# Causal mask by GpSimd and VectorE, two attention value products regrouped: one fused two-layer kernel

## The chip, the cores and the metric

The kernel runs on one core of one Trainium2 chip as a single program. The metric is device time in microseconds (us). Engines are named as in the profile: PE (TensorE matmuls), PEld (its weight loads), DVE (VectorE), ACT (ScalarE), POOL (GpSimd), SP (SyncE, which here only issues DMAs).

## The reference, cut to what matters

Two blocks follow each other on 1024 tokens of width 1024 (plus 16 meta tokens in the first). The first block runs a state space branch (SSD) and a "forgetting attention" (fox) of 16 heads of 64 side by side. The second runs a differential attention (4 heads, values 128 wide) and a dilated attention (8 heads of 64). The change touches the three attentions:

```python
# fox: q, k, v per head; c is the running sum of log forget gates
s = q @ k.T * scale + (c_q[:, None] - c_k[None, :])
s = where(kpos[None, :] <= qpos[:, None], s, -inf)      # causal mask
o = softmax(s) @ v
# differential: two score maps per head, no mask
w = softmax(s0 - slope * dist) - lam * softmax(s1 - slope * dist)
o = w @ v                                               # v is 128 wide
# dilated: windows of dilation 1, 4, 16, merged by their denominators
o = sum over patterns of (window softmax) @ v
```

## The kernel before

All work is hand-ordered: generators yield pieces of attention, and a fixed table (RATIOS, ORDERS, the planner in `merge`) puts projection matmuls between them. Each engine then runs its own instructions strictly in the order written, so a wait of one instruction holds all that is queued behind it on that engine. Projections and scores are split: a fp32 value is held as hi (fp32r, a faster matmul type) plus lo, and a product is two or three fp32r matmuls (`mm3`, L112 to L114, is hi·hi, hi·lo and lo·hi).

Stages in the trace: 0 to 76 us prologue, 76 to 645 fox (8 pairs of heads, some 71 us each with their filler), 645 to 1430 SSD, 1430 to 1815 the merge of the first block, 1815 to 2190 differential (4 heads, some 90 us each), 2190 to 2510 dilated (4 pairs of heads), and then the tail.

An attention loop over eight query tiles i of 128 rows runs as a software pipeline (`pipeline`): `pre(i)`, `A(i+2)`, `C(i-1)`, `B(i)`.

- **A** computes scores. In fox, for each head j of the pair: per bank, matmuls of the hi and lo keys (L566, L567), then a bf16 matmul of an identity with a mask table that adds the causal mask to the last 128 columns (L569), then one DVE instruction that adds the bias `cb` and takes the running minimum into `mn` (L570, printed as CUSTOM_DVE_ANT_0, with a READ_ACCUMULATOR behind it), then the exp on ACT with that minimum as bias (L573), then a copy of 16 columns on POOL (`pm`, L576). Tile i is 16 + 128(i+1) columns wide, N is the tile's scores.
- **B** transposes the tile on PE (L624) and copies it out of PSUM into `pt` (L630 on ACT; fox and differential use ACT, dilated alternates with DVE, L632).
- **C** multiplies by the values. In fox it runs once per four tiles (L604, L607, with the sum taken out by L609). In differential it runs per tile, eight fp32 128x128 matmuls (L1211; each shows as two instructions). In dilated per tile, ten 64-wide fp32 matmuls (L1318) and one of 96 rows (L1319) for leftover columns, which a DVE copy collects into `more` (L1290) and PE transposes (L1301).

In the differential loop `pre(i)` (L1193 to L1195) forms the difference of the two exps of tile i on DVE; A has two 1024-wide reductions (L1173) and two exps (L1176). `vtok` are the values by tokens (L469), evacuated by ACT. The gate `zs` of a fox pair is a projection in the filler that ends in a tanh on ACT (L519) and a product on DVE (L520).

Of the kernel before, what the change touches and what calls it, by code (L numbers as in the profile page):

```python
# [66 lines left out]
class Kern:  # L67
# [128 lines left out]
    def consts(self):  # L196
# [6 lines left out]
        self.identb = cst.tile([128, 128], BF16, name="identb")  # L203
        self.maskb = cst.tile([128, 128], BF16, name="maskb")
        V.tensor_copy(out=self.identb, in_=self.ident)
        V.tensor_copy(out=self.maskb, in_=self.cm[:, 3, :])
# [253 lines left out]
    def v_tokens(self, vT, blocks):  # L460

        nc = self.nc
        v = self.slot("vtok", w=1024)
        vv = v.rearrange("p (b c) -> p b c", c=128)
        for g in range(0, len(blocks), 4):
            ps = self.bank()
            for n, c0 in enumerate(blocks[g:g + 4]):
                nc.tensor.transpose(ps[:, n * 128:(n + 1) * 128], vT[:, c0:c0 + 128], self.ident)
            nc.scalar.activation(out=v[:, g * 128:g * 128 + 512], in_=ps, func=AF.Copy)  # L469
        return vv  # L470
# [67 lines left out]
    def fox_attend(self, p, st):  # L538
# [12 lines left out]
        def A(i):  # L551
# [6 lines left out]
            for j in range(2):  # L558
                N = self.slot("N")
                mn = self.sm.tile([128, 3], F32, tag="mn", name="mn", bufs=4)  # L560
                qt = st["q"][j][:, i * 128:(i + 1) * 128]
                for c in range(n):
                    s0, s1 = c * w, min(W, c * w + w)
                    S = self.bank()[:, :s1 - s0]
                    last = c == n - 1
# [7 lines left out]
                nc.scalar.activation(out=N[:, :W], in_=N[:, :W], func=AF.Exp, scale=-1.0, bias=mn[:, n - 1:n],  # L573
# [41 lines left out]

    def transposes(self, N, off, nb, pts, act=False):

        nc = self.nc
        for g in range(0, nb, 4):
# [5 lines left out]
            self.evac(pts[g // 4][:, :n], ps[:, :n * 128].rearrange("p (b c) -> p b c", c=128), act)  # L625
# [35 lines left out]
    def ssd_chunks(self, g, st):  # L661
# [43 lines left out]
        def prep(c):  # L705
# [7 lines left out]
            cbm = self.sm.tile([128, 128], F32, tag="cbm", name="cbm", bufs=2)  # L713
# [402 lines left out]
    def v_by_tokens(self, n, st):  # L1116
        vT = st.pop("vT")
        st["v"] = self.v_tokens(vT, [128 * b for b in range(8)])
        if n >= 4:
            st["vx"] = self.v_more(vT)  # L1120
            next(st["vx"])
        yield
# [56 lines left out]
    def diff_attend(self, p, st):  # L1179
# [18 lines left out]
        def B(i):  # L1198
            P = Ws.pop(i)
            pt = self.slot("pt", w=1024)  # L1200
            r = pt.rearrange("p (b c) -> p b c", c=128)
            self.transposes(P[0], 0, 8, [r[:, :4], r[:, 4:]], act=True)
            PTs[i] = pt
            return 8 * 109

        def C(i):
            pt = PTs.pop(i)
            if i % 4 == 0:
                O[0] = self.bank()
            for b in range(8):  # L1210
                te.matmul(O[0][:, (i % 4) * 128:(i % 4 + 1) * 128], st["v"][:, b, :], pt[:, b * 128:(b + 1) * 128],  # L1211
                          start=b == 0, stop=b == 7)
            if i % 4 == 3:
                nc.scalar.activation(out=y[:, (i - 3) * 128:(i + 1) * 128], in_=O[0], func=AF.Copy)
            return 8 * 218
# [34 lines left out]
    def dil_attend(self, p, st):  # L1250
# [3 lines left out]
        Ns, PTs, O = {}, {}, [None]  # L1254

        def A(i):
            d = dil_tile(i)
            own = d["own"]
            n0, n1 = own.stop - own.start, d["nrest"]
            Ns[i] = []  # L1260
            for j in range(2):
# [3 lines left out]
                q = st["q"][j][:, i * 128:(i + 1) * 128]  # L1265
# [5 lines left out]
                for c, (at, tab, n) in enumerate(((d["own_at"], d["tab_own"], n0), (d["rest_at"], d["tab_rest"], n1))):  # L1271
# [4 lines left out]
                                     accum_out=self.lall[:, 4 + 2 * p + j, i:i + 1])  # L1276
                Ns[i].append(N)
            return 8 * 145

        def B(i):  # L1280
            d = dil_tile(i)
            if i == 0:
                st["vx"] = next(st["vx"])
            big, small = self.slot("pt", w=1024), self.slot("pt", w=512)
            more = self.sm.tile([128, 128], F32, tag="cbm", name="more", bufs=2)[:, :96]
            for j in range(2):
                N = Ns[i][j]
                x = N[:, 256:688] if d["a"] == 0 else N[:, 0:432]
                e = slice(128, 144) if d["a"] == 0 else slice(0, 16)
                V.tensor_copy(out=more[:, 48 * j:48 * j + 48].rearrange("p (c e) -> p c e", e=16),  # L1290
                              in_=x.rearrange("p (c e) -> p c e", e=144)[:, :, e])
                ps = self.bank()
                for b, (_, c) in enumerate(d["blocks"][:4]):
                    te.transpose(ps[:, b * 128:(b + 1) * 128], N[:, c:c + 128], self.ident)
                self.evac(big[:, j * 512:(j + 1) * 512], ps)
                ps = None
            ps = self.bank()
            c = d["blocks"][4][1]
            for j in range(2):
                te.transpose(ps[:, j * 128:(j + 1) * 128], Ns[i][j][:, c:c + 128], self.ident)  # L1300
            te.transpose(ps[:96, 256:384], more, self.ident)  # L1301
            self.evac(small[:, :256], ps[:, :256])
            self.evac(small[:96, 256:384], ps[:96, 256:384])
            PTs[i] = big, small
# [3 lines left out]
        def C(i):  # L1308
            d = dil_tile(i)
            big, small = PTs.pop(i)  # L1310
            if i % 4 == 0:
                O[0] = self.bank()
            q = slice((i % 4) * 128, (i % 4 + 1) * 128)
# [500 lines left out]
```

## Time and profile before

| what | value |
|---|---|
| median of 3 runs | 2732.16 us (2728.64 to 2733.09) |
| profiled execution, its own time | 2729.51 us |
| its span | 2727.7 us |
| PE busy | 2659.8 us, 98% of the span |
| DVE, ACT, POOL busy | 1372.3, 1165.6, 684.5 us (50%, 43%, 25%) |
| mean granted TensorE clock | 0.994 |

PE takes matmuls one behind the other, and their durations overlap, so the price of a matmul is the distance from its start to the next one's start, not the duration printed. The row of a wait gives in brackets how long the engine was idle and who released it. In `2.85 PE L604 ... x16` sixteen instructions are put together in one row.

### The profile page before, as it was taken

The numbers are of one execution on the slowest core, as the hardware profiler recorded it, in microseconds if no ns is written. First come the engines' busy times: TensorE is split into PE (matmuls) and PEld (weight loads), VectorE is DVE, ScalarE is ACT, GpSimd is POOL, SyncE is SP. The second block draws the span as 40 slices with busy tenths as digits, with TensorE's granted clock in tenths as the row PEclk, the third lists the DMA queues.
The fourth block names the chain that finished last, engine by engine and source line by source line (L and its number), as shares of the span: only waits on it lengthen the run. The fifth ranks groups of instructions, "written<-read, shape, count | busy, mean of one in ns | idle before, by whom it ended". The sixth has DMA issues, their size and how long they took to land. (4 is left out here: it accounts for less than half of the span.)

```text
span 2727.7 us, 38674 instructions
## 1 busy us (share of the span) xinstructions
PE 2659.8 (98%) x14925; PEld 2232.2 (82%) x14925; DVE 1372.3 (50%) x2761; ACT 1165.6 (43%) x2080; POOL 684.5 (25%) x764
## 2 busy tenths in 40 slices
PE   8999999999999999999999999999999999998999
PEld 6888888888989889889877887878877877777877
DVE  5433322233574573654756777444654555446332
ACT  5554444445343433443432123445644555445331
POOL 1112121111243342342432333111111121204321
PEclk9999999999999999999999999999999999998999
DMA  3122222221123123122168653340222223324422
GB/s 131 58 64 72 78 79 71 78 64 62 39 88 114 55 78 116 55 103 91 55 207 279 205 182 131 128 121 30 72 70 70 79 94 94 86 72 146 160 65 70
DMA packets 85464, 266.87 MB, mean 98 GB/s; under 512 B 10880, under 2 KB 12032, under 8 KB 84256
## 3 DMA queue, kind: packets, MB, share of 16 engines
q1 hardware_dynamic: 85280, 264.40, 30.3%
q8 instruction: 117, 1.92, 0.3%
q14 instruction: 67, 0.55, 0.1%
HBM read 205.57 MB, written 33.49 MB: 88 GB/s over the span
## 5 line engine op out<-in xcount | busy, mean ns | idle before, releaser
L121 POOL TENSOR_TENSOR wlo<-wraw,whi 128x1024 fp32r<-128x1024 f32 (+2 forms) x168 | 374.4, 2232 | 1288.7 <-ACT whi L120 1077.8
L112 PE MATMUL bank<-uh,whi 128*128 128x512 f32 (+4 forms) x1752 | 625.8, 357 | 0.1
L114 PE MATMUL bank<-uh,wlo 128*128 128x512 f32 (+4 forms) x1752 | 618.8, 353 | 0.1
L113 PE MATMUL bank<-ul,whi 128*128 128x512 f32 (+4 forms) x1752 | 618.5, 353 | 0.0
L114 PEld LDWEIGHTS bank<-uh,wlo 128*128 128x128 f32 (+1 forms) x1752 | 327.9, 187 | 35.4 <-POOL wlo L121 0.5
L112 PEld LDWEIGHTS bank<-uh,whi 128*128 128x128 f32 (+1 forms) x1752 | 328.3, 187 | 34.3 <-issue 1.1
L113 PEld LDWEIGHTS bank<-ul,whi 128*128 128x128 f32 (+1 forms) x1752 | 328.2, 187 | 32.3
L112 PE MATMUL bank<-u,whi 128*128 128x512 f32 x512 | 207.8, 406 | 0.7 <-ACT pr L935 0.7
L113 PE MATMUL bank<-u,whi 128*128 128x512 f32 x512 | 203.6, 398 | 0.0
L114 PE MATMUL bank<-u,wlo 128*128 128x512 f32 x512 | 203.3, 397 | 0.0
L120 ACT ACTIVATE whi<-wraw 128x1024 fp32r<-128x1024 f32 (+2 forms) x169 | 155.3, 926 | 20.5 <-DMA wraw<-in_w_pa_dram 18.2
L630 ACT ACTIVATE pt<-bank 128x512 f32<-128x512 f32 (+1 forms) x320 | 143.0, 509 | 44.8 <-PE bank L624 38.1
L114 PE MATMUL bank<-yh,wlo 128*128 128x512 f32 x384 | 152.5, 397 | 1.0 <-POOL wlo L121 0.8
L112 PE MATMUL bank<-yh,whi 128*128 128x512 f32 x384 | 152.3, 397 | 0.9 <-ACT whi L120 0.9
L113 PE MATMUL bank<-yl,whi 128*128 128x512 f32 x384 | 151.9, 395 | 0.0
L647 DVE SCALAR_TENSOR_TENSOR acc<-raw,cwh,acc 128x1040 f32<-128x1040 f32 x72 | 93.7, 1302 | 109.5 <-ACT acc L644 107.8
L573 ACT ACTIVATE N<-N,mn 128x272 f32<-128x272 f32 (+7 forms) x128 | 100.3, 786 | 45.2 <-DVE mn L570 44.0
L114 PEld LDWEIGHTS bank<-u,wlo 128*128 128x128 f32 x512 | 97.2, 190 | 23.2
L112 PEld LDWEIGHTS bank<-u,whi 128*128 128x128 f32 x512 | 97.8, 191 | 22.3 <-ACT pr L935 1.1
L113 PEld LDWEIGHTS bank<-u,whi 128*128 128x128 f32 x512 | 97.6, 191 | 20.7
L121 POOL TENSOR_TENSOR wo<-wl,wo 128x512 fp32r<-128x512 f32 x52 | 73.4, 1425 | 157.8 <-ACT wo L120 150.6
L624 PE MATMUL bank<-cm,N 128*128 128x128 f32 x832 | 106.9, 273 | 0.0
(326 smaller groups left out, 4961.5 us busy)
## 6 DMA issues: line engine op xcount, KB each, us to landing
wraw<-in_w_in_dram SPq DMA_DIRECT2D x120, 512.0 KB, 4.1
gt<-d_gate SPq DMA_DIRECT2D x48, 512.0 KB, 5.7
ab<-d_acs SPq DMA_DIRECT2D x32, 512.0 KB, 3.5
qs<-qt SPq DMA_DIRECT2D x48, 256.0 KB, 2.9
wl<-in_w_out_dram SPq DMA_DIRECT2D x48, 256.0 KB, 5.4
tab<-in_tab_dram SPq DMA_DIRECT2D x8, 1056.0 KB, 5.9
cb<-d_csp SPq DMA_DIRECT2D x16, 520.0 KB, 7.6
d_gate<-gt SPq DMA_DIRECT2D x16, 512.0 KB, 2.9
```

Source lines behind the costliest of these rows:

```text
L112: te.matmul(ps, lh, rh, start=start, stop=False)
L113: te.matmul(ps, lh, rl, start=False, stop=False)
L114: te.matmul(ps, ll, rh, start=False, stop=stop)
L120: self.nc.scalar.activation(out=hi, in_=src, func=AF.Copy)
L121: (self.nc.vector if vector else self.nc.gpsimd).tensor_tensor(out=lo, in0=src, in1=hi.bitcast(F32), op=ALU.subtract)
L573: nc.scalar.activation(out=N[:, :W], in_=N[:, :W], func=AF.Exp, scale=-1.0, bias=mn[:, n - 1:n], accum_out=self.lall[:, 2 * p + j, i:i + 1])
L624: nc.tensor.transpose(ps[:, b * 128:(b + 1) * 128], N[:, c:c + 128], self.ident)
L630: self.nc.scalar.activation(out=out, in_=ps, func=AF.Copy)
L647: V.scalar_tensor_tensor(out=acc[:, :L], in0=raw[:, k:k + L], scalar=w(k), in1=acc[:, :L], op0=ALU.mult, op1=ALU.add)
```

## The change

1. **Fox.** The mask matmul L569 and its two bf16 tables go. For each (i, j) POOL now adds the mask to the bias of the last 128 columns beforehand (`cd`, four buffers), and DVE takes the last 128 columns in an instruction of their own with `cd` in place of `cb`.
2. **Differential.** The values and the transposed weights are split into hi and lo: B's evacuation on ACT writes hi, and a DVE subtraction writes lo (in `transposes`, and once per head in `v_tokens`). C runs once per two tiles, as `mm3` on 256 columns, eight blocks of three matmuls.
3. **Dilated.** The tiles come in the order 0, 2, 4, 6, 1, 3, 5, 7; C runs once per four tiles (one half of every class): eight 512-wide fp32 matmuls, eight 128-wide ones, and eight of 96 rows for the leftovers. The `more` copy moves from DVE in B to POOL in A, ahead by two tiles.

```diff
@@ fox_attend, A
+                cd = self.sm.tile([128, 128], F32, tag="cd", name="cd", bufs=4)
+                nc.gpsimd.tensor_tensor(out=cd, in0=cb[j][:, W - 128:W], in1=self.cm[:, 3], op=ALU.add)
...
-                    te.matmul(S, qt, st["k"][j][1][:, s0:s1], start=False, stop=not last)
-                    if last:
-                        te.matmul(S[:, s1 - s0 - 128:], self.identb, self.maskb, start=False, stop=True)
-                    nc.vector.tensor_tensor_reduce(
-                        out=N[:, s0:s1], in0=cb[j][:, s0:s1], in1=S, scale=1.0,
-                        scalar=mn[:, c - 1:c] if c else HUGE, op0=ALU.add, op1=ALU.min, accum_out=mn[:, c:c + 1])
+                    te.matmul(S, qt, st["k"][j][1][:, s0:s1], start=False, stop=True)
+                    ends = [(s0, s1, cb[j][:, s0:s1])] if c < n - 1 else [(s0, s1 - 128, cb[j][:, s0:s1 - 128]),
+                                                                          (s1 - 128, s1, cd)]
+                    for a, b, k in ends:
...
+                        nc.vector.tensor_tensor_reduce(
+                            out=N[:, a:b], in0=k, in1=S[:, a - s0:b - s0], scale=1.0,
+                            scalar=mn[:, m - 1:m] if m else HUGE, op0=ALU.add, op1=ALU.min, accum_out=mn[:, m:m + 1])
@@ transposes
-            self.evac(pts[g // 4][:, :n], ps[:, :n * 128].rearrange("p (b c) -> p b c", c=128), act)
+            x, hi = ps[:, :n * 128].rearrange("p (b c) -> p b c", c=128), pts[g // 4][:, :n]
+            self.evac(hi, x, act)
+            if los:
+                nc.vector.tensor_tensor(out=los[g // 4][:, :n], in0=x, in1=hi.bitcast(F32), op=ALU.subtract)
@@ differential, C
-            for b in range(8):
-                te.matmul(O[0][:, (i % 4) * 128:(i % 4 + 1) * 128], st["v"][:, b, :], pt[:, b * 128:(b + 1) * 128],
-                          start=b == 0, stop=b == 7)
+            for b in range(8):
+                hi, lo = (pt[b // 4][:, x] for x in range(2))
+                v = [x[:, b, :] for x in st["v"]]
+                self.mm3(o, v[0], v[1], hi[:, b % 4], lo[:, b % 4], b == 0, b == 7)
@@ dilated, A
+                nc.gpsimd.tensor_copy(out=Xs[i][:, 48 * j:48 * j + 48].rearrange("p (c e) -> p c e", e=16),
+                                      in_=x.rearrange("p (c e) -> p c e", e=144)[:, :, e])
@@ dilated, C
+            for c in range(4):
+                for j in range(2):
+                    h = slice(64 * j, 64 * j + 64)
+                    te.matmul(O[h], st["v"][:, 2 * c + a, h], pt[j][:, c], start=c == 0, stop=False)
```

**Place 1, POOL in the fourth fox pair, tiles 4 and 5** (cb is the bias, cm the table of constants with the mask, N the tile after its exp, pm the copy). Before:

```order
L576 COPY pm_3142<-N_214_3143 128x16
L576 COPY pm_3142<-N_215_3156 128x16
L576 COPY pm_3142<-N_216_3179 128x16
L576 COPY pm_3142<-N_217_3192 128x16
L576 COPY pm_3142<-N_218_3220 128x16
L576 COPY pm_3142<-N_219_3233 128x16
```

After, at the same place:

```order
L562 TENSOR_TENSOR cd_3253<-cb_3041,cm_107 128x128
L582 COPY pm_3250<-N_214_3251 128x16
L562 TENSOR_TENSOR cd_3268<-cb_3043,cm_107 128x128
L582 COPY pm_3250<-N_215_3266 128x16
L562 TENSOR_TENSOR cd_3293<-cb_3041,cm_107 128x128
L582 COPY pm_3250<-N_216_3291 128x16
```

An add of mask and bias now stands between any two copies, behind the copy of the tile before it.

**Place 2, DVE in the second differential head, tiles 6 and 7** (dist is the bias, ld the factors of the two exps). Before:

```order
L1173 ISA N_17031,mn<-dist,bank_17033 128x1024
...
L1173 ISA N_17040,mn<-dist,bank_17042 128x1024
...
L1193 RECIPROCAL ld<-ld 128x1
L1194 SCALAR_TENSOR_TENSOR ld<-ld,nlam,lall 128x1
L1195 SCALAR_TENSOR_TENSOR N_16988<-N_16997,ld,N_16988 128x1024
L1173 ISA N_17075,mn<-dist,bank_17077 128x1024
```

After, at the same place:

```order
L1183 ISA N_17345,mn<-dist,bank_17347 128x1024
...
L1183 ISA N_17354,mn<-dist,bank_17356 128x1024
...
L635 TENSOR_TENSOR pt<-bank,pt 128x4x128 x2
L1203 RECIPROCAL ld<-ld 128x1
L1204 SCALAR_TENSOR_TENSOR ld<-ld,nlam,lall 128x1
L1205 SCALAR_TENSOR_TENSOR N_17309<-N_17318,ld,N_17309 128x1024
L1183 ISA N_17408,mn<-dist,bank_17410 128x1024
```

The two subtractions of a tile's B (they read the bank and what ACT wrote from it) now stand between the reductions of one tile and the difference of the next.

**Place 3, PE in the first dilated pair** (cm is the identity, pt the transposed weights). Before, between the scores of one tile and the transposes of another:

```order
L1269 MATMUL bank<-qt_18755,qs_18784 128x288
L1318 MATMUL bank<-pt_18995,vtok_18853 64x128 x8
L1318 MATMUL bank<-pt_18996,vtok_18853 64x128 x2
L1319 MATMUL bank<-pt_18996,vx_18982 128x128
L1294 MATMUL bank<-cm,N_18938 128x128 x4
```

After, once per four tiles:

```order
L1287 MATMUL bank<-qt_19211,qs_19240 128x288
L1340 MATMUL bank<-pt,vtok_19309 64x512 x8
L1345 MATMUL bank<-pt_19462,vtok_19309 64x128 x8
L1351 MATMUL bank<-pt_19463,vx_19447 64x128 x8
L1318 MATMUL bank<-cm,N_19526 128x128 x4
```

The value products of four tiles stand together, and between the scores and transposes of the other tiles there is none.

## Rows read from the trace of the kernel before

**Rows 1.** Page, parts 1 and 5: busy time by engine; the exps of fox

```profile
PE 2659.8 (98%) x14925; PEld 2232.2 (82%) x14925; DVE 1372.3 (50%) x2761; ACT 1165.6 (43%) x2080; POOL 684.5 (25%) x764
L573 ACT ACTIVATE N<-N,mn 128x272 f32<-128x272 f32 (+7 forms) x128 | 100.3, 786 | 45.2 <-DVE mn L570 44.0
```

**Rows 2.** Waits of PE: line, waited for, us in total, times, longest

```profile
PE bank L1301 <- DVE more L1290: 9.9, 6, 2.6
...
PE bank L604 <- ACT pt L630: 5.6, 8, 0.8
```

**Rows 3.** Timeline of PE, fourth fox pair: start, us, instruction, wait before

```profile
330.11 0.23 PE L569 MATMUL bank<-maskb,identb 128*128 128x128 bf16 x1
330.15 0.45 PE L566 MATMUL bank<-kx,qs 128*128 128x456 f32 x1
330.44 0.37 PE L567 MATMUL bank<-ky,qs 128*128 128x456 f32 x1
330.64 0.37 PE L566 MATMUL bank<-kx,qs 128*128 128x456 f32 x1
...
332.04 2.85 PE L604 MATMUL bank<-pt,vtok 128*64 128x512 f32 x16 [0.75 <-ACT pt L630]
```

**Rows 4.** Timeline of ACT, the same pair

```profile
324.29 0.60 ACT L519 ACTIVATE zs<-bank 128x512 f32<-128x512 f32 x1 [2.70 <-PE bank L114]
...
330.47 0.94 ACT L573 ACTIVATE N<-N,mn 128x784 f32<-128x784 f32 x1
...
331.40 1.07 ACT L630 ACTIVATE pt<-bank 128x512 f32<-128x512 f32 x2
```

**Rows 5.** Timeline of POOL, the same pair: first and last of ten copies

```profile
318.06 0.20 POOL L576 COPY pm<-N 128x16 f32<-128x16 f32 x1 [3.70 <-ACT N L573]
...
331.56 0.20 POOL L576 COPY pm<-N 128x16 f32<-128x16 f32 x1 [0.73 <-ACT N L573]
```

**Rows 6.** Groups by line and shape: busy us, mean ns, idle before

```profile
L570 DVE CUSTOM_DVE_ANT_0 N<-cb,bank 128x144 f32<-128x144 f32 x16 | 4.8, 303 | 72.6 <-PE bank L569 72.3 <-DMA cb<-d_csp 0.2
...
L761 POOL TENSOR_TENSOR yq<-yq,th 128x128 f32<-128x128 f32 x128 | 60.7, 508 | 124.1 <-DVE yq L758 124.1
...
L695 DVE TENSOR_TENSOR xdd<-xr,xdd 128x512 fp32r<-128x512 f32 x28 | 19.2, 684 | 0.0
```

**Rows 7.** Timeline of DVE, the fourth fox pair

```profile
324.92 0.69 DVE L520 SCALAR_TENSOR_TENSOR zs<-zs,bank 128x512 f32<-128x512 f32 x1 [4.25 <-ACT zs L519]
```

**Rows 8.** Timeline of PE, second differential head: products, transposes, products of the next tile

```profile
1956.55 1.95 PE L1211 MATMUL bank<-pt,vtok 128*128 128x128 f32 x16
1958.34 1.04 PE L624 MATMUL bank<-cm,N 128*128 128x128 f32 x8
...
1961.08 1.95 PE L1211 MATMUL bank<-pt,vtok 128*128 128x128 f32 x16
```

**Rows 9.** Timeline of DVE, the same head

```profile
1958.67 1.28 DVE L1195 SCALAR_TENSOR_TENSOR N<-N,ld,N 128x1024 f32<-128x1024 f32 x1
1960.35 1.22 DVE L1173 CUSTOM_DVE_ANT_0 N<-dist,bank 128x1024 f32<-128x1024 f32 x1 [0.39 <-PE bank L1171]
```

**Rows 10.** Timeline of ACT, the same head

```profile
1959.49 1.06 ACT L630 ACTIVATE pt<-bank 128x512 f32<-128x512 f32 x2
1961.67 1.15 ACT L1176 ACTIVATE N<-N,mn 128x1024 f32<-128x1024 f32 x1 [1.12 <-DVE mn L1173]
```

**Rows 11.** Timeline of PE, second dilated pair: one tile's products, next transposes

```profile
2302.56 1.31 PE L1318 MATMUL bank<-pt,vtok 128*64 128x128 f32 x20
2303.80 0.49 PE L1319 MATMUL bank<-pt,vx 96*128 96x128 f32 x2
2304.13 1.04 PE L1294 MATMUL bank<-cm,N 128*128 128x128 f32 x8
```

**Rows 12.** Windows: us, busy of PE, PEld, DVE, ACT, POOL, granted clock, DMA share, GB/s

```profile
2376.00:2378.90 2.90, 0.86 (x4) 0.66 (x4) 2.13 (x6) 0.77 (x3) 2.90 (x5) 1.00 0.67 178
2379.00:2382.40 3.40, 3.40 (x10) 2.93 (x11) 1.10 (x4) 1.86 (x5) 2.62 (x14) 0.52 0.68 222
```

More of the change, by code (lines that the diff above doesn't have):

```diff
@@ L458, in move_k, with v_tokens @@
             self.nc.sync.dma_start(out=st[1][o:p, :n].bitcast(F32), in_=st[0][a:b, :n].bitcast(F32))
-    def v_tokens(self, vT, blocks):
+    def v_tokens(self, vT, blocks, split=False):
         nc = self.nc
-        v = self.slot("vtok", w=1024)
-        vv = v.rearrange("p (b c) -> p b c", c=128)
+        vs = [self.slot("vtok", F32R if split else F32, 1024) for _ in range(1 + split)]
+        v = vs[0]
         for g in range(0, len(blocks), 4):
@@ L468, in v_tokens @@
                 nc.tensor.transpose(ps[:, n * 128:(n + 1) * 128], vT[:, c0:c0 + 128], self.ident)
-            nc.scalar.activation(out=v[:, g * 128:g * 128 + 512], in_=ps, func=AF.Copy)
-        return vv
+            c = slice(g * 128, g * 128 + 512)
+            nc.scalar.activation(out=v[:, c], in_=ps, func=AF.Copy)
+            if split:
+                nc.vector.tensor_tensor(out=vs[1][:, c], in0=ps, in1=v[:, c].bitcast(F32), op=ALU.subtract)
+        vs = [x.rearrange("p (b c) -> p b c", c=128) for x in vs]
+        return vs if split else vs[0]
     def v_meta(self, vT):
@@ L614, in fox_attend, with transposes @@
         nc.sync.dma_start(out=self.d_yatt[p], in_=y)
-    def transposes(self, N, off, nb, pts, act=False):
+    def transposes(self, N, off, nb, pts, act=False, los=None):
         nc = self.nc
@@ L1117, in v_by_tokens @@
         vT = st.pop("vT")
-        st["v"] = self.v_tokens(vT, [128 * b for b in range(8)])
+        st["v"] = self.v_tokens(vT, [128 * b for b in range(8)], n < 4)
         if n >= 4:
@@ L1260, in A @@
             Ns[i] = []
+            Xs[i] = self.sm.tile([128, 128], F32, tag="cbm", name="more", bufs=4)[:, :96]
             for j in range(2):
@@ L1278, in A @@
             return 8 * 145
         def B(i):
-            d = dil_tile(i)
+            t, d = order[i], dil_tile(order[i])
+            r, a = t // 2, t % 2
             if i == 0:
                 st["vx"] = next(st["vx"])
-            big, small = self.slot("pt", w=1024), self.slot("pt", w=512)
-            more = self.sm.tile([128, 128], F32, tag="cbm", name="more", bufs=2)[:, :96]
-            for j in range(2):
[L1287 to L1291, printed above, removed]
+            if r == 0:
+                PTs[a] = ([self.ph.tile([128, 4, 512], F32, tag="pt", name="pt", bufs=2) for _ in range(2)],
+                          self.slot("pt", w=1024), self.slot("pt", w=512))
@@ L1305, in B @@
+            self.evac(own.rearrange("p (j c) -> p j c", j=2)[:, :, q], ps[:, :256].rearrange("p (j c) -> p j c", j=2))
+            self.evac(more[:96, q], ps[:96, 256:384])
             del Ns[i]
@@ L1308, in C @@
         def C(i):
[L1309 to L1313, printed above, removed]
[L1314 to L1324 removed]
+            if i % 4 != 3:
+                return 0
+            a = order[i] % 2
+            pt, own, more = PTs.pop(a)
+            O = self.bank()
+            for c in range(4):
+                for j in range(2):
+                    h = slice(64 * j, 64 * j + 64)
+                    te.matmul(O[h], st["v"][:, 2 * c + a, h], pt[j][:, c], start=c == 0, stop=False)
+            for r in range(4):
+                q = slice(128 * r, 128 * r + 128)
+                for j in range(2):
+                    h = slice(64 * j, 64 * j + 64)
+                    te.matmul(O[h, q], st["v"][:, 2 * r + 1 - a, h], own[:, j * 512 + 128 * r:j * 512 + 128 * r + 128],
+                              start=False, stop=False)
+            for r in range(4):
+                q = slice(128 * r, 128 * r + 128)
+                t = 2 * r + a
+                for j in range(2):
+                    te.matmul(O[64 * j:64 * j + 64, q], st["vx"][:96, t * 128 + 64 * j:t * 128 + 64 * j + 64], more[:96, q],
+                              start=False, stop=r == 3)
+            nc.scalar.activation(out=by_class(y)[:, :, 128 * a:128 * a + 128], in_=O.rearrange("p (r s) -> p r s", r=4),
+                                 func=AF.Copy)
+            return 5300
         yield from self.pipeline(8, A, B, C)
```

72 lines of the change are left out of this document (34 added, 38 removed).

## Prediction

> **What bounds the kernel now.** I read the busy shares first: PE works for 2659.8 us of the span, DVE for half of it, ACT and POOL for less [rows 1]. PE is in order, so the time is what PE has to do plus the few places where it waits. The table of PE's waits comes second: two of its larger entries lie in the code that is changed, the 9.9 us of the dilated transposes of `more` behind the DVE copy and 5.6 us, eight times up to 0.8, of fox's C behind the evacuation on ACT [rows 2]. The timelines of the three attention loops come last, since averages over the span hide them: the reader is to see there that in the dense stretch of a fox pair the copies on POOL follow each other at (331.56 - 318.06) / 9 = 1.50 us [rows 5], that ACT has exp and evacuation back to back [rows 4], and that C already starts late behind them [rows 3]. So ACT's and DVE's cadence is at the limit inside a stretch, however low their averages are, and anything that stretches the chain there is paid by PE.
>
> **Part 1, fox, on PE.** A mask matmul takes 0.04 us to the next start, and the fp32r matmul behind it 0.29 where its like takes 0.20 [rows 3]: about 0.13 where scores follow, and I take 0.05 where transposes or filler follow, since the step back to fp32r is paid there anyway. Half of the 128 masks stand at each: 64 x 0.13 + 64 x 0.05 = 11 us less for PE, 1.4 per pair.
>
> **Part 1, on POOL, DVE and ACT.** POOL now takes add, copy, add, copy strictly (place 1). A copy waits for the exp of its own (i, j); the next add waits behind it, though all its inputs are long there; the last reduction on DVE needs the add, the exp needs the reduction. So what ran side by side on three engines becomes one chain. A step from copy to copy: the copy 0.20 [rows 5], the add, a hop to DVE, the reduction of 128 columns, a hop to ACT, the exp, and a hop to POOL. The add has no row here. Its nearest is a two-input 128x128 operation on POOL, 0.508 [rows 6]; below, a copy of 16 columns at 0.20 bounds it. I take 0.51, as shape, type count and engine are the same. The reduction is 0.30, that of the 144-column form [rows 6]. From a reduction's end to the exp is 1961.67 - (1960.35 + 1.22) = 0.10 [rows 9, 10]; from an exp's end to the copy 331.56 - (330.47 + 0.94) = 0.15 [rows 4, 5], and I take the same from POOL to DVE. Sum: 0.20 + 0.51 + 0.15 + 0.30 + 0.10 + 0.15 = 1.41 us plus the exp.
>
> [...]
>
> An exp of 784 columns takes 0.94 [rows 4]; the mean over the eight widths (592 columns) is 0.786 [rows 1], so 0.10 per tile. From tile 1's first copy to tile 5's last, nine steps hold exps of 0.54 + 2 x (0.64 + 0.74 + 0.84 + 0.94) = 6.86. The chain is 9 x 1.41 + 6.86 = 19.55 us where the trace shows 13.50: 6.05 more. Behind tile 3 the filler's gate stands in both queues, a tanh of 0.60 on ACT and a product of 0.69 on DVE [rows 4, 7]; with a late chain they fall between two of its steps, about 1.4 with a hop. C stands behind the evacuations, and these stand behind tile 5's exps on ACT: it slips by 7.45. What is left of the mask saving outside this stretch is 0.2. Per pair 7.25, in eight pairs **+58 us**. Tiles 6 and 7 have filler behind them, which hides their part of the chain. Bounds: an add at 0.30 and no detour give 4.5 with the slack that PE's own work leaves, an unhidden tail 10 per pair: +36 to +80.
>
> **Part 2, differential, on PE.** A tile's value product takes 1958.34 - 1956.55 = 1.79 us [rows 8]. The new one, for two tiles, is 24 fp32r matmuls of 256 columns; 456 columns take 0.20 [rows 3], so 256 take 0.115, 2.8 for two tiles against 3.58. Sixteen times 0.8 is 12 us less.
>
> **Part 2, on DVE and ACT.** A subtraction reads PSUM and is 512 wide, nearest 0.684 [rows 6]; there are 64 of them for the weights and 8 for the values, 49 us of DVE. Alone that would hide. But their place decides (place 2): they stand ahead of `pre` and of the next reductions, and wait for ACT's evacuation, which stands behind two exps of the later tile. One turn: reduction to exp 1.32 [rows 9, 10], two exps 2.3, two evacuations 1.06 [rows 10], a hop of 0.1, the last subtraction 0.68, `pre` 1.28 for its long part [rows 9] and about 0.4 for two instructions of one column ahead of it: 7.1 us. Now a turn takes 1961.08 - 1956.55 = 4.53 [rows 8], and PE's work would be 4.1. Wherever two turns follow without filler, the difference of up to 3 us falls on PE. Laying out one head by hand with the filler that the order has, I get waits of 1.45, 1.85, 0.75, 2.25 and 3.5 us, near 10, against 3 saved: +7 per head, **+28 us** for four. Bounds 4 to 9 per head, +16 to +36, as filler hides more or less.
>
> **Part 3, dilated.** Four tiles' products are now 4 x (2304.13 - 2302.56) = 6.3 us [rows 11]. New: 16 instructions of 512 columns at 0.23 (0.20 x 512 / 456 [rows 3]), and 32 of 128 columns at 1.24 / 20 = 0.062 [rows 11], 3.7 + 2.0 = 5.7. Eight times 0.6 is 5 us less. The `more` copies go to POOL two tiles ahead, so the 9.9 us of waits [rows 2] go; what ends last there next is the reductions themselves. Against that: between the scores of tile i + 2 and the transposes of B the product of 1.57 is missing, which covered reductions and exps; two turns per pair lose up to that, I take 1.1, 9 us in all. And C comes right behind the last scores and waits for evacuations that stand behind their exps, about 1.2 each time, 10 us. Sum: -5 - 10 + 9 + 10 = **+4 us**, bounds -15 to +20. Per tile POOL has as many copies as DVE had, and nothing else of the chain; they cost nothing, hidden by the two tiles of lead.
>
> **The clock.** After a stretch in which PE worked 0.86 of 2.90 us the granted clock fell to 0.52 for 3.4 us [rows 12], which costs half of that, 1.7. This kernel falls so few times, since it rarely waits. The new waits are of 2 us and more, once per fox pair and once or more per differential head: 12 x 1.7 = **+20 us**. Not every wait must end so (the wait of 0.75 before C [rows 3] comes in every fox pair [rows 2], and the mean clock of the whole run is 0.99): 0 to 40.
>
> [...]
>
> **The sum** against the profiled execution: 2729.5 + 58 + 28 + 4 + 20 = 2839.5; the median of the runs lies 2.7 above it, so **2842 us**.
>
> **Rivals.** (a) *The waits stay hidden.* Then PE's work alone counts: -11 - 12 - 5 - 10 = 2694 us, faster. It holds if a step on POOL, DVE and ACT takes no longer than the 1.50 us of now, that is if copy, add, hops and reduction together take 0.74 beside a mean exp of 0.76, half of the 1.41 above. C's wait behind ACT [rows 3], with no such chain yet, speaks against it. 5 in 100. (b) *The chain holds, but at the low bounds*: adds near 0.3, no detour, no clock falls, the dilated part a gain: +36 + 16 - 8 = 2776. [...] 18 in 100. (c) *The clock falls at each burst and stays low*: the waits spread over several places of a stretch, so PE works at 0.5 for the matmuls of a whole stretch; 20 more for the falls and upper bounds in fox (+22): 2885. 12 in 100. (d) *Gains and losses cancel* within 0.2%: needs fox at +20 and no other loss, 2 in 100.
>
> **How the numbers follow.** The forecast with its own spread (2800 to 2870) has 63 in 100. The range 2766 to 2892 takes in (b) and (c) in their greater part and leaves out (a) and (d). About 0.2%, 5 us, is what a measurement of this kernel can tell from no change. Faster 0.05, same 0.02, slower 0.93.
>
> **What would show it.** In the changed kernel's trace POOL's adds should sit idle "behind" an exp: the wait of the copy (L582) on ACT directly ahead of each add, and copies 2.1 us apart or more in the dense stretch. C of each fox pair's first group should start some 7 us later against the pair's start, with PE waiting for banks from DVE (the reductions) or for `pt`. In a differential head PE should wait in front of C and B for `pt` from the subtraction L635, with turns near 7 us. In the dilated loop the wait behind `more` should be gone and C should wait for ACT. Fox wrong: copies at 1.5 us. Differential wrong: turns of 4.1 to 4.5. The whole is wrong if PE's busy time falls by 30 us and its waits don't grow.

## The result and the profile after

The changed kernel takes 2852.9 us (median of four runs, 2849.5 to 2855.3) where the kernel before takes 2731.6: a ratio of 1.0445, 95% interval 1.0426 to 1.0463. It is 121 us slower. The forecast was 2842 in a range of 2766 to 2892.

The stages, each from the start of the first score matmul of an attention on PE to the start of the next one (read from the two traces; "alone" is the part by itself on the kernel before, from the experiments below):

| stage, us | before | after | change | forecast, with its share of the clock term | the part alone |
|---|---|---|---|---|---|
| up to fox | 75.8 | 77.4 | +1.6 | | |
| fox, first to last score | 569.4 | 625.3 | +55.9 | +58 and +14 | 625.4 |
| SSD and merge | 1191.9 | 1190.8 | -1.1 | 0 | |
| differential | 357.3 | 399.2 | +41.9 | +28 and +7 | 403.3 |
| dilated, first to last score | 305.7 | 325.5 | +19.8 | +4 for this and the tail | 325.1 |
| tail | 227.6 | 234.1 | +6.5 | | 232.3 |

The page of the changed kernel, part 1 (busy time, share of the span, instructions), and the rows of PE's waits (line, waited for: us in total, times, longest) that answer to [rows 1] and [rows 2]:

```profile
PE 2687.4 (94%) x14349; PEld 2215.0 (78%) x14349; DVE 1442.8 (51%) x3023; ACT 1172.8 (41%) x2080; POOL 751.2 (26%) x956
```

```profile
PE bank L631 <- DVE N L1205: 24.7, 9, 4.0
PE bank L610 <- ACT pt L640: 14.0, 8, 2.2
PE bank L568 <- DVE mn L575: 13.2, 15, 1.9
...
PE bank L631 <- DVE mn L575: 9.8, 8, 1.4
PE bank L112 <- DVE mn L575: 9.5, 8, 1.2
...
PE bank L1340 <- ACT pt L640: 6.4, 4, 1.6
PE bank L267 <- DVE lall L1411: 6.3, 1, 6.3
```

PE has 576 instructions fewer and was to be busy for some 28 us less. It is busy for 28 us more, in part because matmuls now run at the low clock (a mean granted clock of 0.981 in place of 0.994), and it waits: for DVE's difference before the transposes of a differential head (L631 for L1205), for the evacuations before fox's C (L610, 14.0 us against 5.6 in [rows 2]), for DVE's reductions, which hold the banks (L568, L631, L112 for L575), and for the evacuations before the four-tile product of the dilated pairs (L1340). The waits for the reductions in fox are 32.5 us in these rows; before, there was one:

```profile
PE bank L566 <- DVE mn L570: 1.4, 1, 1.4
```

The wait for `more` of [rows 2] is gone.

**Fox.** POOL in the fourth pair (start, us, instruction, wait before), the first two copies, the two around the gate and the last two of the stretch of [rows 5]:

```profile
342.01 0.20 POOL L582 COPY pm<-N 128x16 f32<-128x16 f32 x1 [1.96 <-ACT N L579]
342.16 0.45 POOL L562 TENSOR_TENSOR cd<-cb,cm 128x128 f32<-128x128 f32 x1
343.71 0.20 POOL L582 COPY pm<-N 128x16 f32<-128x16 f32 x1 [1.10 <-ACT N L579]
...
351.19 0.20 POOL L582 COPY pm<-N 128x16 f32<-128x16 f32 x1 [1.31 <-ACT N L579]
351.35 0.46 POOL L562 TENSOR_TENSOR cd<-cb,cm 128x128 f32<-128x128 f32 x1
354.92 0.20 POOL L582 COPY pm<-N 128x16 f32<-128x16 f32 x1 [3.12 <-ACT N L579]
...
359.09 0.20 POOL L582 COPY pm<-N 128x16 f32<-128x16 f32 x1 [1.53 <-ACT N L579]
359.24 0.46 POOL L562 TENSOR_TENSOR cd<-cb,cm 128x128 f32<-128x128 f32 x1
361.23 0.20 POOL L582 COPY pm<-N 128x16 f32<-128x16 f32 x1 [1.53 <-ACT N L579]
```

Ahead of every add of this stretch POOL is idle until an exp has ended; the add needs nothing of it and only stands behind the copy that does. From the first copy to the last it is 19.22 us (13.50 in [rows 5]). The end of it on ACT and on PE, answering to [rows 4] and the last row of [rows 3]:

```profile
360.12 0.95 ACT L579 ACTIVATE N<-N,mn 128x784 f32<-128x784 f32 x1 [1.10 <-DVE mn L575]
...
361.07 1.06 ACT L640 ACTIVATE pt<-bank 128x512 f32<-128x512 f32 x2
```

```profile
361.70 2.64 PE L610 MATMUL bank<-pt,vtok 128*64 128x512 f32 x14 [2.12 <-ACT pt L640]
```

C starts 28.8 us behind the pair's first score (332.9), where it took 22.9 before (309.1 to 332.04): 5.9 late, as much as the chain grew.

**Differential.** DVE in the second head, two turns (a turn is from the first reduction L1183 of one tile to that of the next), then ACT's evacuation and PE's transposes there; they answer to [rows 8] to [rows 10]:

```profile
2026.84 1.21 DVE L1183 CUSTOM_DVE_ANT_0 N<-dist,bank 128x1024 f32<-128x1024 f32 x1
...
2030.99 1.29 DVE L635 TENSOR_TENSOR pt<-bank,pt 128x512 fp32r<-128x512 f32 x2 [1.79 <-ACT pt L640]
...
2032.64 1.28 DVE L1205 SCALAR_TENSOR_TENSOR N<-N,ld,N 128x1024 f32<-128x1024 f32 x1
2033.84 1.21 DVE L1183 CUSTOM_DVE_ANT_0 N<-dist,bank 128x1024 f32<-128x1024 f32 x1
```

```profile
2030.38 1.06 ACT L640 ACTIVATE pt<-bank 128x512 fp32r<-128x512 f32 x2
```

```profile
2027.07 1.06 PE L631 MATMUL bank<-cm,N 128*128 128x128 f32 x8 [2.00 <-DVE N L1205]
...
2041.47 1.09 PE L631 MATMUL bank<-cm,N 128*128 128x128 f32 x8 [3.99 <-DVE N L1205]
```

The turn is 2033.84 - 2026.84 = 7.00 us. DVE has nothing to do for 1.79 of them: the subtraction waits for an evacuation that stands behind two exps, and the difference L1205, whose inputs are long there, stands behind the subtraction. PE pays 2.00 and 3.99 us for it.

**Dilated.** PE in the second pair: the scores of the last tile ahead of the first four-tile product, that product, a filler transpose, and the second product:

```profile
2417.49 0.40 PE L1287 MATMUL bank<-qs,qs 128*128 128x288 f32 x1 [0.95 <-DVE mn L1290]
...
2420.76 5.35 PE L1340 MATMUL bank<-pt,vtok 128*64 128x512 f32 x16 [1.59 <-ACT pt L640]
...
2457.67 0.28 PE L267 MATMUL bank<-cm,rsv 128*32 128x128 f32 x1 [2.50 <-DVE rsv L242]
...
2466.24 3.65 PE L1340 MATMUL bank<-pt,vtok 128*64 128x512 f32 x16
```

The first product waits 1.59 and then takes 5.35 us, the second, with filler ahead of it, 3.65.

**The clock.** Windows of the changed kernel (length, busy time of PE, PEld, DVE, ACT and POOL, granted clock, DMA share, GB/s): the fourth fox pair, the fifth, and two pieces of the fifth, 1.00 being the full clock:

```profile
332.90:415.20 82.30, 75.78 (x449) 64.25 (x448) 26.55 (x104) 36.49 (x80) 21.05 (x45) 1.00 0.23 65
415.20:500.10 84.90, 79.53 (x449) 67.02 (x448) 26.56 (x104) 36.59 (x80) 21.04 (x45) 0.94 0.22 65
428.00:431.40 3.40, 3.40 (x10) 2.65 (x9) 2.05 (x11) 1.78 (x6) 1.03 (x4) 0.51 0.00 0
441.80:448.60 6.80, 5.69 (x15) 3.52 (x16) 4.13 (x19) 4.50 (x9) 1.81 (x6) 0.50 0.20 72
```

Both pairs run the same 449 instructions on PE. The clock falls in every second pair alone (the first, third, fifth and seventh), and that pair takes 84.90 in place of 82.30: the fall costs 2.6 us, and without it a pair costs 82.30 - 76.65 = 5.65 us more than before. Before, the granted clock is 1.00 through the whole of fox and of the differential heads.

### The profile page after: what moved, and what is told of

It is laid out like the page before. It is cut to its first block, busy times and chain, and to the rows that moved or that the text cites. A ratio compares the mean times of both kernels' runs of the same rounds, so it can differ in the third digit from the quotient of the medians.

```text
span 2852.3 us, 38099 instructions
## 1 busy us (share of the span) xinstructions
PE 2687.4 (94%) x14349; PEld 2215.0 (78%) x14349; DVE 1442.8 (51%) x3023; ACT 1172.8 (41%) x2080; POOL 751.2 (26%) x956
## 5 line engine op out<-in xcount | busy, mean ns | idle before, releaser
L112 PE MATMUL bank<-uh,whi 128*128 128x512 f32 (+4 forms) x1752 | 627.7, 358 | 9.6 <-DVE mn L575 9.5
L112 PEld LDWEIGHTS bank<-uh,whi 128*128 128x128 f32 (+1 forms) x1752 | 329.8, 188 | 46.0 <-issue 10.9
L112 PE MATMUL bank<-u,whi 128*128 128x512 f32 x512 | 213.4, 417 | 1.2 <-ACT pr L945 0.7
L113 PE MATMUL bank<-u,whi 128*128 128x512 f32 x512 | 209.5, 409 | 0.0
L114 PE MATMUL bank<-u,wlo 128*128 128x512 f32 x512 | 209.3, 409 | 0.0
L112 PE MATMUL bank<-yh,whi 128*128 128x512 f32 x384 | 151.6, 395 | 0.0
L640 ACT ACTIVATE pt<-bank 128x512 f32<-128x512 f32 (+2 forms) x320 | 142.2, 508 | 20.7 <-PE bank L631 18.0
L631 PE MATMUL bank<-cm,N 128*128 128x128 f32 x832 | 108.4, 275 | 34.8 <-DVE N L1205 24.7
L631 PEld LDWEIGHTS bank<-cm,N 128*128 128x128 f32 x832 | 94.6, 141 | 44.3 <-issue 22.1
L112 PEld LDWEIGHTS bank<-u,whi 128*128 128x128 f32 x512 | 101.6, 198 | 24.5 <-ACT pr L945 1.1
L113 PEld LDWEIGHTS bank<-u,whi 128*128 128x128 f32 x512 | 100.8, 197 | 21.8
```

Of the source, the lines that this page charges most:

```text
L112: te.matmul(ps, lh, rh, start=start, stop=False)
L113: te.matmul(ps, lh, rl, start=False, stop=False)
L114: te.matmul(ps, ll, rh, start=False, stop=stop)
L631: nc.tensor.transpose(ps[:, b * 128:(b + 1) * 128], N[:, c:c + 128], self.ident)
L640: self.nc.scalar.activation(out=out, in_=ps, func=AF.Copy)
```

## Do the three parts add up?

Each part was put on the kernel before by itself; the edits are the parts of the diff shown above (fox_only: the first hunk; diff_only: the splits and the differential C; dil_only: the rest).

> Only part 1 (mask by POOL and DVE) on the kernel before; differential and dilated code as before. Theory of the parts that add up: the fox stage of the changed kernel ran 55.9 us longer from the first scores to the last (569.4 to 625.3), so this kernel is at 2731.6 + 56 = 2788 us, with pair periods of 82.3 to 85 against 76.65. Rival, that the loss in fox comes partly from the other parts (buffers, clock): under 2775 us.

Measured: 2787.9 us beside 2733.3 for the kernel before on the same chip, +54.6, with a fox stage of 625.4 us and pairs of 82.3 and 85.0 in turn, as in the changed kernel.

> Only part 2 (differential values' product split) on the kernel before. Parts that add up: the stage from the first differential scores to the first dilated ones was 41.9 us longer in the changed kernel, so 2731.6 + 42 = 2773 us, heads of 99 us against 90. Rival, that the clock falls in it come only with the others: 2765 us or less.

Measured: 2780.4, +47, the stage 403.3. It is 4 us longer alone than with the others: the granted clock is at some 0.5 for 37.5 us of the stage here, for 20.5 us in the changed kernel (a mean granted clock of 0.95 and 0.97).

> Only part 3 (dilated order, products of four tiles, leftover copy on POOL) on the kernel before. Parts that add up: 19.7 us in the stage and 6.5 in the tail behind it, 2731.6 + 26 = 2758 us, with the clock low at the first product of every pair. Rival, that the differential stage's late end caused part of it: 2745 us or less.

Measured: 2755.3, +22, the stage 325.1 and the tail 232.3. The tails of other runs scatter by some 3 us, so of the tail's +6.5 in the changed kernel about half is certain. The four kernels with part 3 have in their tail the wait that reads L267 behind `lall` above (6.3 us there, 5.35 to 6.85 in all four); none of the others has it.

54.6 + 47 + 22 = 124 us, against 121 for all three. In sum the parts don't help or hamper each other, and the clock falls in each part alone as well: the rivals of these three runs fall.

These and most of the runs below are single ones, and the times of the kernel before scatter from 2728.6 to 2736.0 us. The stages in the traces repeat better: where its code is that of before, fox takes 569.4 us in eight traces, the differential stage 357.3 to 358.3 in nine, the dilated one 303.1 to 307.5 in eight. Small differences are read from them.

## Fox: the place of the add, and then DVE

The add is moved ahead, with six buffers in place of four, and nothing else:

```diff
-                cd = self.sm.tile([128, 128], F32, tag="cd", name="cd", bufs=4)
-                nc.gpsimd.tensor_tensor(out=cd, in0=cb[j][:, W - 128:W], in1=self.cm[:, 3], op=ALU.add)
+                cd = cds.pop((i, j))
...
+            for t in range(3) if i == 0 else range(i + 2, min(8, i + 3)):
+                masked(t)
```

> As fox_only, but the adds of mask and bias of a tile are issued on POOL two tiles ahead of its scores (six buffers in place of four), so that no add stands behind the copy of the tile before. The number of instructions on every engine is that of fox_only. Theory of the chain through POOL: the nine steps between copies fall from 19.2 us back to about 14, the pair period to 76 to 78 us, the time to 2722 to 2745 us. Rival, that the extra reduction of 128 columns on DVE (about 0.4 us each, 128 of them) sets the pace: steps stay near 1.9 us or above, pair periods over 80, time over 2760 us.

Measured: 2749.4 us, so 38.5 of the 54.6 us go. Pairs take 78.6 us, and the nine steps between copies 15.5. That is the chain through POOL, shown by an edit that leaves the amount of work on every engine as it was. But the time lies above the expected band (the nine steps were to fall to about 14), and 16 us of loss remain although PE has some 11 us less to do. The groups of this run by line and shape (busy us, mean ns, idle before) show the extra instruction on DVE, and PE's waits what ends last (C's wait, 5.6 us before):

```profile
L580 DVE CUSTOM_DVE_ANT_0 N<-cd,bank,mn 128x128 f32<-128x128 f32 x128 | 44.5, 347 | 18.6
```

```profile
PE bank L615 <- ACT pt L641: 12.4, 8, 1.6
```

So I tried a form in which DVE keeps its old instructions: POOL writes, a tile ahead, a copy of the last bank's bias with the mask in it.

```diff
+            x = ce[i, j] = self.ph.tile([128, 456], F32, tag="ce", name="ce", bufs=2)
+            nc.gpsimd.tensor_copy(out=x[:, :W - 128 - s0], in_=cb[j][:, s0:W - 128])
+            nc.gpsimd.tensor_tensor(out=x[:, W - 128 - s0:W - s0], in0=cb[j][:, W - 128:W], in1=self.cm[:, 3], op=ALU.add)
...
-                        out=N[:, s0:s1], in0=cb[j][:, s0:s1], in1=S, scale=1.0,
+                        out=N[:, s0:s1], in0=ce.pop((i, j))[:, :s1 - s0] if last else cb[j][:, s0:s1], in1=S, scale=1.0,
```

> Part 1 in another form: POOL writes, one tile ahead, a copy of the bias of a tile's last bank with the mask added (one copy and one add per (i, j)), so DVE keeps the number and widths of the kernel before's reductions, no mask matmul on PE, and the pm copies of a tile stand behind the adds of the next. fox_ahead took 19.9 us more in the fox stage than before (589.3 against 569.4), although PE does 11 us less. Theory that those 20 to 30 us are the extra reductions on DVE: the stage falls to 558 to 563 us, the time to 2720 to 2727. Rival, that any work of POOL beside DVE in this stage slows it (DVE's own reductions get longer) or POOL's queue is late: 575 us or more in the stage, 2737 or more.

Measured: 2735.8 (before 2731.7), the stage 572.6. Against fox_ahead 16.7 us of the stage go, so the extra reductions were most of the rest. But neither theory's number came: PE is rid of the masks and the stage is not shorter than the 569.4 of before. DVE's reductions are as long as they were (456 columns take 690 ns in this trace and 689 before), so POOL's work beside them doesn't slow them. POOL's queue isn't out of it, though: DVE waits 24 times for `ce`, 20.2 us in all. Of the 3.2 us over the kernel before, 2.6 stand in the first pair, where the clock falls for 3.4 us. What was missing was an answer to whether PE's work counts in this stretch at all. That needs a run with no mask of any kind:

```diff
-                    te.matmul(S, qt, st["k"][j][1][:, s0:s1], start=False, stop=not last)
-                    if last:
-                        te.matmul(S[:, s1 - s0 - 128:], self.identb, self.maskb, start=False, stop=True)
+                    te.matmul(S, qt, st["k"][j][1][:, s0:s1], start=False, stop=True)
```

> The kernel before with the 128 mask matmuls left out and nothing in their place (the causal mask is missing from the result). PE has 11 us less to do in fox, and DVE, ACT and POOL have what they had. Theory that the dense stretch of a fox pair is paced by DVE and ACT already before the change, so that work taken from PE there only becomes waiting: the stage stays at 567 to 570 us (before 569.4), C's wait behind ACT grows from 0.75 to about 1, time 2729 to 2732. Rival, that PE paces it and that the mended masks lost through POOL: 558 to 561 us in the stage, time 2719 to 2723.

Measured: 2728.3 us, a stage of 566.5, just under the first theory's band: 2.9 us of PE's 11 become time. The 11 are there: from the matmul ahead of each mask to the second one behind it, waits left out, the steps are 10.9 us shorter in sum. By pairs, the first is 1.4 us longer (the clock falls in it for 3.4 us), and from the third on each is 0.5 to 0.6 us shorter (76.05 to 76.14 in place of 76.61 to 76.70), of 1.3 that the steps at the masks give. PE's wait of C on ACT (us in total, times, longest), beside 5.6 in [rows 2]:

```profile
PE bank L601 <- ACT pt L627: 7.5, 8, 1.0
```

So more than half of what PE is spared doesn't come through, as the first theory had it, and C of the fourth pair starts only 0.38 us earlier behind the first score (22.52, 22.90 before). But it isn't nothing, and PE is idle for only 10.1 us of the stage (7.0 before): that DVE and ACT alone pace it is not shown. What is shown is the price. Taking the mask off PE was worth 2.9 us in this run, and some 4 us if the first pair's fall of the clock is left out.

## Differential: where the subtraction stands

The subtractions are left out, with PE's products as in the changed kernel:

```diff
-            self.transposes(P[0], 0, 8, hi, True, lo)
+            self.transposes(P[0], 0, 8, hi, True)
...
-                self.mm3(o, v[0], v[1], hi[:, b % 4], lo[:, b % 4], b == 0, b == 7)
+                self.mm3(o, v[0], v[1], hi[:, b % 4], zero, b == 0, b == 7)
```

> As diff_only, but the 64 subtractions that form the low part of the transposed weights are left out and a tile of zeros stands in for it, so PE does the same matmuls on the same schedule and the low part of the weights is missing from the result. Theory that the subtraction's place on DVE (behind ACT's evacuation, ahead of the next difference and reductions) makes the loss: the stage falls from 403 to 343 to 352 us, heads near 87, time 2717 to 2727 us. Rival, that the products of two tiles at once (C later, bunched, behind more) or the clock make it: the stage stays over 375 us, time over 2750.

Measured: 2728.4 us (before 2731.7), the stage 354.7. All of the loss is in the subtractions; the products of two tiles at once and the clock are no cause by themselves. But the gain of 12 us that PE's products promise isn't there either: the stage is 2.6 us shorter than before (357.3 to 354.7), where the expectation had 5 to 14. The products do take 11.3 us less (45.8 in place of 57.1, waits left out), but PE waits 16.2 us in the stage in place of 9.9, and in the last head, which is 1.3 us longer than before, the clock falls for 3.4 us. The other three heads are 1.0 to 1.5 us shorter.

Then the same subtractions in another place, behind the next tile's difference (and, for a head's last tile, behind its transposes):

```diff
             V.scalar_tensor_tensor(out=P[0], in0=P[1], scalar=l[:, 1:2], in1=P[0], op0=ALU.mult, op1=ALU.add)
             Ws[i] = P
+            self.subtract_late()
```

> As diff_only, with the same instructions, but the two subtractions of a tile stand behind the difference of the next tile instead of ahead of it. A turn on DVE and ACT should fall from 7.1 us to what DVE itself has to do, 2.4 + 1.4 + 1.7 = 5.5 us, and B no longer waits for a difference that stands behind the evacuation: the loss of 46 us falls to 10 to 30, time 2742 to 2762 us. Rival, that the amount of DVE work and not its place counts: within 8 us of diff_only, 2772 or more.

Measured: 2741.5 us, just below the expected band, the stage 366.9. The loss is 9.8 us against the kernel before on the same chip, where diff_only's was 47.0: 37 of the 47 us go by place alone (36.4 by the stages). DVE of this run in the second head, two reductions and the subtraction between them:

```profile
1960.36 1.21 DVE L1187 CUSTOM_DVE_ANT_0 N<-dist,bank 128x1024 f32<-128x1024 f32 x1
...
1964.51 1.29 DVE L638 TENSOR_TENSOR pt<-bank,pt 128x512 fp32r<-128x512 f32 x2
1965.71 1.21 DVE L1187 CUSTOM_DVE_ANT_0 N<-dist,bank 128x1024 f32<-128x1024 f32 x1
```

The turn is 1965.71 - 1960.36 = 5.35 us, close to the 5.5 of DVE's own work, and the subtraction waits for nothing here (the next turn takes 5.85, with a wait of 0.63). That is still over the 4.53 of [rows 8], but the rest of the loss isn't there: this head takes 89.96 us, 90.04 before. It is in the other three, with 90.2, 91.6 and 95.2 us in place of 87.2, 90.0 and 90.1, and these are the ones in which the granted clock falls (0.98, 0.98 and 0.96 over the head, 1.00 in the second). Why it falls in them and not in the second, no run here shows.

## Dilated: one good edit and one dear one

The leftover copy alone, on the kernel before:

```diff
-                V.tensor_copy(out=more[:, 48 * j:48 * j + 48].rearrange("p (c e) -> p c e", e=16),
-                              in_=x.rearrange("p (c e) -> p c e", e=144)[:, :, e])
+                nc.gpsimd.tensor_copy(out=Xs[i][:, 48 * j:48 * j + 48].rearrange("p (c e) -> p c e", e=16),
+                                      in_=x.rearrange("p (c e) -> p c e", e=144)[:, :, e])
```

> Only the move of the leftover copy to POOL, ahead by two tiles, on the kernel before (order of tiles and products as before). The waits of the leftover transposes, 9.9 us, go: 2720 to 2725 us, with 296 to 300 us in the dilated stage in place of 305.7. Rival, that another wait at the same place (the exp, the next reduction) takes their place: 2729 us or more.

> The kernel before with the leftover copy on POOL alone, once more with repeats, since the single run was 6 us (0.22%) below the kernel before. If the move is worth the 8.3 us that the dilated stage lost in that trace, 2722 to 2727 us against 2731 to 2733; if that was the scatter of single runs, no difference.

This kernel also has four small buffers in place of two, which copies two tiles ahead need. Measured: 2725.8 in the single run, and as the median of six 2724.1 us (2722.4 to 2727.2) beside 2733.1: a ratio of 0.9967, 95% interval 0.9955 to 0.9979. The dilated stage is 297.4 and 296.9 us in place of 305.7. The waits for `more` are gone. The stage is 8.3 and 8.8 us shorter, and 7.2 of the 8.8 are idle time of PE (15.2 us in place of 22.5). What is left at that place is PE's wait for the evacuation ahead of L1319, 3.2 us of it behind the last score, in the tail (us in total, times, longest, in the repeated run):

```profile
PE bank L1319 <- ACT pt L630: 4.2, 5, 2.0
```

This kernel is faster than both, by 0.3% against the kernel before. It also says what the rest of part 3, the new order and the product of four tiles, costs: dil_only's stage is 325.1, so 28 us, although PE has 280 instructions fewer in it. PE is idle for 31.1 us of dil_only's stage and for 15.2 of this one's; the other 12 us are busy time, at a mean granted clock of 0.94 in place of 0.97. One piece of filler ahead of the first product in place of behind it tests the wait there (the costs that its neighbours give the planner are set so that only this piece moves):

```diff
-            return 5300
+            return 5300 if i == 7 else 0
...
+            if i == 4:
+                yield 7660
             if i:
                 yield C(i - 1)
```

> As dil_only, with one piece of filler (twelve projection matmuls, 2.8 us, and the small transpose behind them) standing ahead of the first four-tile product of each pair in place of behind the transposes that follow it. Theory that this product comes before its evacuations are through (1.6 to 1.7 us of wait) and that the wait brings the low clock in which it then runs (5.18 us for its 512-wide part in place of 3.48): 2 to 3.4 us less per pair, 8 to 13 us in all, 2742 to 2747 us. Rival, that DVE's backlog in the stretch is the limit and the wait only moves on: within 3 us of dil_only's 2755.

Measured: 2751.7 us, 3.6 less than dil_only, which is less than the expected 8 to 13 and hardly outside the rival's 3. The stage is 6.0 less, the tail 2.7 more (235.0 us). In the second and third pair the theory holds: they take 95.4 and 95.5 us in place of 98.4 and 98.7. The same product in the second pair, first in dil_only, then in dil_fill:

```profile
2321.32 5.35 PE L1325 MATMUL bank<-pt,vtok 128*64 128x512 f32 x16 [1.58 <-ACT pt L630]
```

```profile
2322.84 3.65 PE L1325 MATMUL bank<-pt,vtok 128*64 128x512 f32 x16
```

The wait of 1.58 us and the 1.7 that the low clock added (5.35 in place of 3.65) both go. In the first pair only the wait was there and the gain goes into two new ones (0.65 and 0.32); in the last pair there is no filler to move, and its product still waits 1.60 and runs slowly. So this cause is shown for about 3 us in each of two pairs. The other waits are named by the trace of the changed kernel and were not tried: L1287 behind the reductions (0.95 above), the filler transpose L267 behind DVE (2.50 above; 0.64 at the like place before), and in the last pair 6.3 us of L267 behind DVE, which stands ahead of the last product and is counted in the tail.

## All three, mended

fox_bank, diff_lo_late and dil_fill together (with three instead of four of the small `more` buffers):

> All three parts, each with its cause mended: the masked bias of a last bank written ahead by POOL (fox_bank), the subtractions behind the next difference (diff_lo_late), the filler ahead of the first dilated product (dil_fill). If the causes are the ones named and add up: 2731.7 + 4 + 10 + 12 = 2758 us, where the changed kernel takes 2853. Rival, that parts hamper each other or that a cause is missing: 2780 us or more.

Measured: 2765.4 us, with stages of 572.6, 367.1 and 317.2 us. 87 of the 121 us are gone, by edits of place and order, and in fox also by 128 reductions fewer on DVE with 128 copies on POOL in their place. It lies 7 us above the sum, since dil_fill gave less than was counted: the three runs by themselves are 4.0, 9.8 and 18.6 us over the kernel before, and this one is 32.4 over it, which is their sum. Its fox stage is 3.2 us over before, the differential 9.8, the dilated 11.5 and the tail 9.8. It is still slower than the kernel before: no part but the leftover copy has a gain to set against what is left.

## Why the prediction was right, and where it wasn't

- **What bounds the kernel.** Right in the main: a longer chain through POOL, DVE and ACT is paid by PE. That the dense stretch is at the limit of ACT and DVE is half right by fox_nomask: PE spared of the masks wins less than half of them. The 11 us of masks and 12 us of products were counted in full, in the sum and in rival (a), 2694 us; 2.9 and 2.6 us of them become time, so that rival's price was wrong by some 17 us even if no chain had come. Rival (c) adds up to 2884, not 2885.
- **The chain in fox.** The mechanism was right in every link. The step was 1.41 us beside the exp in the forecast and is 1.18 in the trace: 343.71 - 342.01 = 1.70 with an exp of 0.52. Durations laid end to end count too much: the add starts 0.15 behind the copy's start, not 0.20, takes 0.45, not 0.51, and the reduction starts 0.03 behind the add's end (342.64), not 0.15. The detour by the gate was 1.4 in the forecast; the copy behind it comes 3.73 us after the last (351.19 to 354.92, first tile after the gate) where its neighbours are about 2.0 apart: 1.7. Per pair 7.25 was forecast, 5.65 was measured without the clock. Eight times 5.65 is 45; the measured 55.9 are these and the clock's 10.6.
- **The add's price.** 0.51 from the nearest row, 0.45 to 0.46 measured (0.458 in the median of 128), so the nearest row was a usable guide. An add at 0.30, as the lower bound of the fox term and rival (b) have it, is shown by no run; the shortest of the 128 in the changed kernel takes 0.452.
- **The turn in differential.** 7.1 forecast, 7.00 measured. Before the products and transposes of the second head PE waits at four places where the layout by hand had five: 1.1, 2.0, 0.9 and 4.0 us, 8.0 against near 10. The stage grew by 41.9, the forecast was 28 and 7 for the clock. The term that was off is the product's gain, 12 us counted in full; diff_lo_zero shows 2.6. With 2.6 in its place the sum is 28 + 9 + 7 = 44.
- **Dilated.** The term furthest off: +4 forecast (and bounds -15 to +20), +20 in the stage and up to 6 in the tail. The 10 us won by the leftover copy were right (8.3 and 8.8). The new order and products were to cost -5 + 9 + 10 = 14 and cost 28. C's wait was 1.2 eight times in the forecast; it was 1.6 four times, where no filler stands ahead of it. What failed is the clock: the forecast gave this stage none of it, and 12 of the 28 us are busy time at a lower granted clock, in three of the four pairs just on the 512-wide matmuls (5.24 and 5.35 us in place of 3.65). Missing too were the filler's waits for DVE (2.5 us in place of 0.6 to 0.8 in each of three pairs, and the 6.3 in the tail).
- **The clock.** Forecast 12 falls of 1.7 us, one for each fox pair and differential head. The fox pairs fall every second time and for 3.4 and 6.8 us, costing 2.6; each differential head once, the last one twice. In the differential heads of the changed kernel a fall stands at the wait of 4.0 us in each, in the last head at one of 2.6 too, and the waits of 2.0 brought none there. In fox the same instructions with the same waits (1.22 and 1.23 us ahead of the fall at 428.0 in the fifth pair, 1.23 and 1.22 at that place in the fourth) brought it down in one pair and not in the next, so which gap counts can't be told from the gap alone in these runs. The 40 at the upper end, which rival (c) takes as well, is shown by no run for these two stages: in fox the falls cost the 10.6 above, and in the differential stage they last 20.5 us at some 0.5, which is worth 10 at most (an estimate: half of their length).

On the whole 110 us were forecast against 121, by mechanisms that the runs bear out, but that the sum came so close is in part luck, since the terms err both ways: fox with its share of the clock had 16 us too much, differential 7 too little, the dilated stage and the tail 22 too little.

## What to carry to other kernels

An instruction with its inputs ready isn't free on an idle engine: ask what stands ahead of it in that engine's own queue, and whom that waits for. In fox and in the differential heads some 36 us each, well over half of either loss, came back by moving instructions without removing one. And before counting a saving on the busiest engine, ask whether it is the pacing engine in that stretch: on an engine that is busy for 98% of the span, 11 us of work left out gave 2.9 and 11.3 us gave 2.6, and a run that simply leaves the work out prices the saving before anything is built.

## What was not expected of the hardware

The same sequence of a fox pair alternates, from the second pair on, between 82.3 us at full clock and 84.9 to 85.0 with 10.2 us of low clock (6.8 in one pair), in two kernels (the changed one and fox_only). A wait of 0.75 us before C (before the change) brought no fall; in dil_only a wait of 1.58 us before the dilated product did in the second pair and not in the first, in the changed kernel in the first and not in the third. POOL's adds and copies beside DVE's reductions in fox_bank left those at 690 ns (689 before).
